# Three short products ahead of six chunks, and activations without a shifted low part, in a hybrid decoder layer

## The chip, the cores and the metric

The kernel runs on one core of one Trainium2 chip. The metric is the device time of one execution in microseconds. Three runs of the kernel before gave a median of 1507.69 us (1507.61 to 1507.84).

## What is computed

One decoder layer on 256 positions of width 2048, in float32: a norm, one wide input projection, two branches, a merge, an output projection, and a gated MLP, with a final norm.

```python
h = rms_norm(x, ln1)
qkv_a, beta_a, decay_a, z_a, qkv_b, gate_a, gate_b = split_columns(h @ w_in)
y_a = gated_deltanet(qkv_a, beta_a, decay_a, z_a, ...) @ w_branch_a      # 8 heads of 128, chunks of 64
q_b, k_b, v_b = jnp.split(qkv_b, 3, axis=-1)                             # 8 heads of 128, partial rotary
y_b = moba_attention(q_b, k_b, v_b) @ w_branch_b                         # causal over the one block of 256
merged = sigmoid(gate_a) * y_a + sigmoid(gate_b) * y_b
x = x + merged @ w_out
h = rms_norm(x, ln2)
u = causal_dwconv(h @ w_up, ffn_conv, ffn_conv_bias)                     # 2 x 5632 columns
u_gate, u_val = jnp.split(u, 2, axis=-1)
x = x + (silu(u_gate) * u_val) @ w_down
return rms_norm(x, final_norm)
```

## The kernel before

Activations lie transposed: features on the 128 partitions, the 256 positions along the free dimension, so that a 2048-wide activation is 16 tiles (k = 0 to 15) of 128 x 256. All large products are made from split numbers: a value is kept as a high part of the reduced float32 type and a low part that holds the rest. For each k three products are added up: high weights by high activation, high weights by low activation, low weights by high activation (the loop in `block`, L188 to L193; L110 is the instruction).

Weights come by one DMA queue (SyncE) in pieces of 1 MB into four raw buffers (`wraw`). ScalarE casts them to the high part (`wh`, L120), VectorE subtracts to get the low part (`wl`, L117), in two pieces of 1024 columns each. There are two buffers of each part. A *block* is 128 output columns: 16 k, 48 products of 256 columns. A *chunk* is two blocks (j = 0 and 1) into one PSUM tile, 96 products. The stages that are made of chunks are, in the order of time: the input projections of the delta rule (`ps_gdn`, `ps_z`), of the attention (`ps_moba`), the gates (`ps_gate`, 16 chunks), the two branch projections (`ps_br`, 16 chunks of half the length, as k runs to 7 alone), the output projection (`ps_wo`, 8 chunks), and the up-projection (`ps_up`, 44 chunks). The values of the attention (`ps_v`) and the down-projection (`pd`) have the activations as weights and stream 512 columns of the matrix.

While the chunks of the first stages run, small products of the delta rule and of the attention are put between them: `main_mm` counts the cost of the large products, and each time it comes to 1700 (`EVERY`) it lets each background item go one step on (`tick`). The place of these steps in TensorE's order depends on that count alone, not on time. In gate chunk 2 the last item ends; from there to the end TensorE runs the stages one after the other, with the two sums of squares of the second norm (`R2`, L98) between the output projection and the second chunk of the up-projection.

Where things lie is set by hand. `Parts` (L152 to L171) holds an activation as one row of elements: for each group of 8 k the high and low parts alternate, 256 elements each, and 64 elements are left over at the end of a group. `at(k, a)` gives the place of part `a` of tile `k`; the low part (a = 1) of the last k of a group (7 and 15) is moved on by `TURN` = 40 elements. `load_w` cuts the weights out of a buffer of 2048 + 64 elements from an offset `at`: 24 for most stages, and what `PLACE` says for two of them (8 for `ps_v`, 16 for `ps_wo`). The addresses of the built program, in bytes: the weights of the chunks start 32 past a multiple of 64, those of the output projection at a multiple of 64. The activations `hc`, `yca`, `ycb` and `h2` start 32 past a multiple of 64 too, the merged activations `mc` at a multiple of 64.

Of the kernel before, what the change touches and what calls it, by code (L numbers as in the profile page):

```python
# [11 lines left out]
F32 = mybir.dt.float32  # L12
# [7 lines left out]
P = 128  # L20
T = 256
D = 2048
KD = D // P
# [3 lines left out]
NF = DFF // P  # L27
EPS = 1e-6
EVERY = 1700
PLACE = {"v": 8, "wo": 16}  # L30
TURN = 40
GROUP = 8
ATT_SCALE = 128 ** -0.5
CONST_FIELDS = [
# [48 lines left out]
def layer_kernel(ctx: ExitStack, tc: tile.TileContext, xT, pos, cst, csel, ceye, vec, convw, ffw, bdv,  # L83
                 w_gdn, w_bd, w_moba, w_mv, w_gate, w_ba, w_bb, w_o, w_up, w_dn, fnorm, out):
    nc = tc.nc
    pe, act, dve, pool, sp = nc.tensor, nc.scalar, nc.vector, nc.gpsimd, nc.sync
# [5 lines left out]
    def r3(t, b):  # L92
        return t.rearrange("p (a b) -> p a b", b=b)
# [25 lines left out]
    def split(hi, lo, src):  # L119
        act.copy(hi, src)  # L120
        return low(hi, lo, src)
# [6 lines left out]
    def fetch(src, n=2048):  # L128
        raw = wpool.tile([P, 2048], F32, name="wraw", tag="wraw", bufs=4)
        sp.dma_start(raw[:, :n], src)  # L130
        return raw

    def load_w(src, n=2048, into=None, piece=1024, raw=None, at=0):
        raw = raw or fetch(src, n)
        wh, wl = into or [wpool.tile([P, 2048 + 64], F32R, name=t, tag=t)[:, at:at + 2048] for t in ("wh", "wl")]
        for o in range(0, n, piece):
            lows.append(split(wh[:, o:o + piece], wl[:, o:o + piece], raw[:, o:o + piece]))
        return wh[:, :n], wl[:, :n]
# [13 lines left out]
    class Parts:  # L152
# [6 lines left out]
        def at(self, k, a):  # L159
            return k // GROUP * self.size + (2 * (k % GROUP) + a) * T + TURN * (a and k % GROUP == GROUP - 1)  # L160

# [20 lines left out]
    def mmt(name):  # L182
        return pst[0].tile([P, 2, T], F32, name=name, tag="mm")

    def sdt(name):
        return pst[1].tile([P, 512], F32, name=name, tag="sd")

    def block(ps, j, w, x, kt, k0=0, k1=None):  # L188
        wh, wl = (r3(t, P) for t in w)
        for k in range(k0, k1 or kt):  # L190
            for w_, a in ((wh, 0), (wh, 1), (wl, 0)):
                main_mm(ps[:, j], w_[:, k, :], x.one(k, a), j == k == a == 0 and w_ is wh,
                        k == kt - 1 and w_ is wl)  # L193

    def chunk(blocks, x, kt, name, raws=(None, None), piece=1024, steps=((0, 0, None), (1, 0, None))):
        ps = mmt("ps_" + name)
        ws = {}
        for j, k0, k1 in steps:
            if j not in ws:
                ws[j] = load_w(blocks[j], kt * P, raw=raws[j], piece=piece, at=PLACE.get(name, 24))  # L200
            block(ps, j, ws[j], x, kt, k0, k1)
        return ps

    def join(dst, ps, r):
        with tc.high_priority():
            dve.tensor_tensor(dst, ps, r, op=ALU.mult)  # L206

    def scaled(xv, lnv, k, x):
        for j in range(xv.shape[1]):
            act.activation(x.one(k + j, 0), xv[:, j, :], AF.Identity, scale=lnv[:, k + j:k + j + 1])  # L210
            dve.scalar_tensor_tensor(x.one(k + j, 1), xv[:, j, :], lnv[:, k + j:k + j + 1],
                                     x.one(k + j, 0).bitcast(F32), op0=ALU.mult, op1=ALU.subtract)
# [9 lines left out]
    def both(r):  # L222
        return r[:, None, :].to_broadcast([P, 2, T])
# [3 lines left out]
    hc = Parts(hp, KD, "hc", tag="hc")  # L227
# [31 lines left out]
    raws = [fetch(w) for w in (w_gdn[2], w_gdn[3])]  # L259
# [18 lines left out]
    sp.dma_start(eye, ceye)  # L278

    ps_k0 = chunk([w_gdn[2], w_gdn[3]], hc, KD, "gdn", raws)  # L280


# [18 lines left out]
    R1b = both(R1)  # L301
# [21 lines left out]
    m = m_st.enter_context(tc.tile_pool(name="m", bufs=2, reuse_waits="tile"))  # L323
# [275 lines left out]
    def pair(w, i):  # L599
        return [w[2 * i], w[2 * i + 1]]  # L600

    for gr in range(4):
        h0 = 2 * gr
        kq = g.tile([P, 2, 2, T], F32, name="kq", bufs=1)
        v = g.tile([P, 2, T], F32, name="v", bufs=1)
        for a, t in enumerate((kq[:, 1], kq[:, 0], v)):
            if gr == 0 and a < 2:
                ps = (ps_q0, ps_k0)[a]
            else:
                ps = chunk(pair(w_gdn, 4 * gr + a), hc, KD, "gdn")  # L610
            conv4(t, ps, 8 * a + h0)
            if gr == 0 and a == 1:
                bg.append(decay())
        yv = ya[:, h0:h0 + 2, :]
        join(yv, chunk(pair(w_gdn, 4 * gr + 3), hc, KD, "z"), R1b)
        act.activation(yv, yv, AF.Silu)
        while gr == 0 and bg:
            tick()
        bg.append(gdn(h0, kq, v))
        if gr == 3:  # L620
            bg.append(rotary())
            sp.dma_start(ffv, ffw)
# [46 lines left out]
    for gr in range(4):  # L669
        h0 = 2 * gr  # L670
        qk = []
        for a in range(2):
            ps = chunk(pair(w_moba, 2 * gr + a), hc, KD, "moba")
# [3 lines left out]
        if gr % 2 == 0:  # L677
            ps = [mmt("ps_v").rearrange("p a b -> p (a b)") for _ in range(2)]
            for q_ in range(4):
                wh, wl = (r3(t, 512) for t in load_w(w_mv[2 * gr + q_], at=PLACE["v"]))  # L680
                for i in range(2):
# [9 lines left out]
        v = v4[:, :, (gr % 2) * T:(gr % 2 + 1) * T]  # L691
# [8 lines left out]

    gts = gp.tile([P, 16, 2, T], F32, name="gts")
    for c in range(16):
        join(gts[:, c], chunk(pair(w_gate, c), hc, KD, "gate"), R1b)
        act.activation(gts[:, c], gts[:, c], AF.Sigmoid)
    while bg:
        tick()
# [10 lines left out]

    m_st = ExitStack()
    m = m_st.enter_context(tc.tile_pool(name="mp", bufs=1, reuse_waits="tile"))
    mc = Parts(m, KD, "mc")  # L720
    for c in range(8):
        bts = [yp.tile([P, 2, T], F32, name="bt", bufs=3) for _ in range(2)]
        join(bts[0], chunk(pair(w_ba, c), yc[0], H, "br"), gts[:, c])
        ps = chunk(pair(w_bb, c), yc[1], H, "br")
# [18 lines left out]
    h2 = Parts(hp, KD, "h2", tag="hc")  # L743
    for c in range(8):
        steps = ((0, 0, KD - 2), (1, 0, 8), (0, KD - 2, KD), (1, 8, KD))
        ps = chunk(pair(w_o, c), mc, KD, "wo", **({} if c else dict(piece=512, steps=steps)))
        if c % 2 == 0:
            s = slice(2 * c, 2 * c + 4)
            sp.dma_start(x1[:, s, :], xT[:, s, :])
        xc = x1[:, 2 * c:2 * c + 2, :]  # L750
        dve.tensor_tensor(xc, xc, ps, op=ALU.add)
        scaled(xc, ln2v, 2 * c, h2)
        if c == 0:
            act.activation(sqa, xc, AF.Square)
        else:
            sq = b.tile([P, 2, T], F32, name="sq2")
            act.activation(sq, xc, AF.Square)
            if c < 7:
                pool.tensor_tensor(sqa, sqa, sq, op=ALU.add)
# [6 lines left out]
    ak = bk.enter_context(tc.tile_pool(name="ak", bufs=1, side="right", reuse_waits="tile"))  # L766
    acts = ak.tile([P, NF, T], F32, name="acts")
    for c in range(NF):
        ps = chunk([w_up[c], w_up[NF + c]], h2, KD, "up")
        un = b.tile([P, 2, T], F32, name="unf")  # L770
        join(un, ps, R2b)
        t = b.tile([P, 2, T], F32, name="cvf")
        for j in range(2):
            w = ffv[:, j * NF + c, :]
            act.activation(t[:, j, :], un[:, j, :], AF.Identity, scale=w[:, 2:3], bias=w[:, 3:4])
            for d in (1, 2):
                dve.scalar_tensor_tensor(t[:, j, d:], un[:, j, :T - d], w[:, 2 - d:3 - d], t[:, j, d:],
                                         op0=ALU.mult, op1=ALU.add)
        sg = b.tile([P, T], F32, name="sg")
        act.activation(sg, t[:, 0, :], AF.Silu)  # L780
        pool.tensor_tensor(acts[:, c, :], sg, t[:, 1, :], op=ALU.mult)
# [128 lines left out]
```

## Time and profile before

| | |
|---|---|
| runs, median (range) | 1507.69 us (1507.61 to 1507.84) |
| profiled execution, its own time | 1512.56 us |
| its span, first to last instruction | 1510.8 us |
| TensorE products (PE), busy | 1494.0 us, 99% |
| VectorE / ScalarE / GpSimd busy | 968.2 / 721.1 / 121.1 us |
| moved by DMA | 277.23 MB, mean 184 GB/s |
| granted TensorE clock | 0.995 |

PE is the product on TensorE, PEld the load of its weights. Matmuls are pipelined, so the duration of a product (some 280 ns) is longer than the step from one start to the next; steps are read from the start times. In the timeline, products of the same form that follow each other stand in one row with their number (x2). In the chain of waits a piece is a stretch of one engine's work with nothing waited for between, with its start, its length and its number of instructions. "wh", "wl" are the high and low weights, "hc", "h", "mc", "yca", "ycb" the activations.

### The profile page before, as it was taken

What the parts mean: (1) busy time and instruction counts of PE and PEld (TensorE: products, weight loads), DVE (VectorE), ACT (ScalarE), POOL (GpSimd) and SP (SyncE); (2) the same over time, 40 slices, a digit from 0 to 9 for tenths busy, and PEclk for the clock granted to TensorE, in tenths of its full rate; (3) what the DMA queues carried; (4) which work ended last, traced back from release to release, by engine and by line L of the source; (5) the groups of instructions that cost most, each with busy time, mean ns of one, the idle gap of its engine ahead of it and who ended that gap; (6) DMA issues with size and microseconds to landing.
All of it is one profiled execution on the core that took longest, in us unless ns stands there. A gap on an engine that the chain in (4) does not pass through costs nothing.

```text
span 1510.8 us, 26931 instructions
## 1 busy us (share of the span) xinstructions
PE 1494.0 (99%) x11471; PEld 1434.1 (95%) x11471; DVE 968.2 (64%) x1373; ACT 721.1 (48%) x948; POOL 121.1 (8%) x133
## 2 busy tenths in 40 slices
PE   9999999999999999999999999999999999999998
PEld 8999999998999999999999999999999998888886
DVE  7988695886665445666666666666666665555554
ACT  5655363434474433445455444454444554444444
POOL 0001011042120000110100000000000000000000
PEclk9999999999999999999999999999999999999999
DMA  9445444444336553568555555555555554555552
GB/s 341 171 148 184 171 153 162 152 158 144 136 126 209 195 182 125 183 215 303 195 171 195 193 195 187 183 189 196 195 184 184 192 195 167 195 196 195 195 195 84
DMA packets 45657, 277.23 MB, mean 184 GB/s; under 512 B 5504, under 2 KB 6992, under 8 KB 15456
## 3 DMA queue, kind: packets, MB, share of 16 engines
q1 hardware_dynamic: 43712, 270.98, 52.0%
q0 software_dynamic: 960, 2.36, 0.5%
q10 hardware_dynamic: 864, 2.16, 0.4%
q8 instruction: 90, 1.47, 0.4%
q14 instruction: 31, 0.25, 0.0%
HBM read 271.68 MB, written 3.80 MB: 182 GB/s over the span
## 4 chain that ended last, share of the span: by engine, by line
PE 90%; DVE 5%; ACT 2%; DMA 1%; issue 1%; SPq 0%; DVEq 0%; POOLq 0%; ACTq 0%
PE ps_up L110 32%; PE pd L98 16%; PE ps_gate L110 11%; PE ps_gdn L110 8%; PE ps_wo L110 6%; PE ps_br L110 5%; PE ps_moba L110 3%; PE ps_z L110 3%; PE ps_v L110 2%; DVE wl L117 2%; ACT wh L120 1%; DMA wraw<-in_w_gdn 1%; PE g L98 1%; PE py L552 0%; PE pu L558 0%
## 5 line engine op out<-in xcount | busy, mean ns | idle before, releaser
L117 DVE TENSOR_TENSOR wl<-wraw,wh 128x1024 fp32r<-128x1024 f32 (+1 forms) x500 | 607.1, 1248 | 221.6 <-ACT wh L120 221.0
L120 ACT CAST wh<-wraw 128x1024 fp32r<-128x1024 f32 (+1 forms) x500 | 497.5, 1040 | 481.2 <-PE ps_up L110 171.8
L110 PE MATMUL ps_up<-h,wh 128*128 128x256 f32 x2816 | 489.7, 279 | 0.0
L110 PEld LDWEIGHTS ps_up<-h,wh 128*128 128x128 f32 x2816 | 429.4, 189 | 0.1
L110 PE MATMUL ps_up<-h,wl 128*128 128x256 f32 x1408 | 392.4, 279 | 0.0
L110 PEld LDWEIGHTS ps_up<-h,wl 128*128 128x128 f32 x1408 | 264.3, 188 | 0.0
L110 PE MATMUL ps_gate<-hc,wh 128*128 128x256 f32 x1024 | 181.2, 281 | 0.0
L110 PEld LDWEIGHTS ps_gate<-hc,wh 128*128 128x128 f32 x1024 | 157.5, 190 | 0.0
L110 PE MATMUL ps_gate<-hc,wl 128*128 128x256 f32 x512 | 143.5, 281 | 0.2 <-DVE wl L117 0.2
L98 PE MATMUL pd<-wl,ah 128*128 128x512 f32 x336 | 130.8, 389 | 0.0
L98 PE MATMUL pd<-wh,al 128*128 128x512 f32 x336 | 130.8, 389 | 0.0
L110 PE MATMUL ps_gdn<-hc,wh 128*128 128x256 f32 x704 | 126.7, 283 | 0.0
L110 PEld LDWEIGHTS ps_gdn<-hc,wh 128*128 128x128 f32 x704 | 108.9, 191 | 0.9 <-ACT wh L120 0.4
L110 PE MATMUL ps_gdn<-hc,wl 128*128 128x256 f32 x352 | 99.8, 284 | 0.8 <-DVE wl L117 0.8
L110 PEld LDWEIGHTS ps_gate<-hc,wl 128*128 128x128 f32 x512 | 96.8, 189 | 0.4 <-DVE wl L117 0.4
L98 PE MATMUL pd<-wh,ah 128*128 128x512 f32 x336 | 92.8, 391 | 0.0
L110 PE MATMUL ps_moba<-hc,wh 128*128 128x256 f32 x512 | 92.8, 282 | 0.0
L206 DVE TENSOR_TENSOR unf<-ps_up,R 128x512 f32<-128x512 f32 x44 | 30.4, 691 | 95.7 <-PE ps_up L110 95.7
L110 PE MATMUL ps_wo<-mc,wh 128*128 128x256 f32 x512 | 89.2, 279 | 0.0
L110 PEld LDWEIGHTS ps_moba<-hc,wh 128*128 128x128 f32 x512 | 78.5, 189 | 0.2
L110 PEld LDWEIGHTS ps_wo<-mc,wh 128*128 128x128 f32 x512 | 78.1, 189 | 0.0
L98 PEld LDWEIGHTS pd<-wh,al 128*128 128x128 f32 x336 | 63.1, 188 | 13.2
(420 smaller groups left out, 1963.5 us busy)
## 6 DMA issues: line engine op xcount, KB each, us to landing
wraw<-in_w_up SPq DMA_DIRECT2D x88, 1024.0 KB, 4.9
wraw<-in_w_dn SPq DMA_DIRECT2D x44, 1024.0 KB, 4.9
wraw<-in_w_gate SPq DMA_DIRECT2D x32, 1024.0 KB, 4.9
wraw<-in_w_gdn SPq DMA_DIRECT2D x30, 1024.0 KB, 5.0
wraw<-in_w_moba SPq DMA_DIRECT2D x16, 1024.0 KB, 4.9
wraw<-in_w_o SPq DMA_DIRECT2D x16, 1024.0 KB, 5.3
wraw<-in_w_mv SPq DMA_DIRECT2D x8, 1024.0 KB, 5.0
wraw<-in_w_ba SPq DMA_DIRECT2D x16, 512.0 KB, 3.5
```

The source lines that it names most:

```text
L98: pe.matmul(ps, a, b, start=(start and i == 0), stop=(stop and i == n - 1), **kw)
L110: pe.matmul(ps, a, b, start=start, stop=stop, skip_group_check=True)
L117: return (eng or dve).tensor_tensor(lo, src, hi.bitcast(F32), op=ALU.subtract)
L120: act.copy(hi, src)
L206: dve.tensor_tensor(dst, ps, r, op=ALU.mult)
```

## The change

Three things are changed.

`TURN` becomes 0: the low part of the tiles 7 and 15 lies where the others do, right behind its high part. The 64 spare elements stay.

A tile of 8 elements is allotted ahead of the merged activations, so that `mc` starts 32 bytes later, and the output projection loses its entry in `PLACE`, so that its weights start at element 24 in place of 16, also 32 bytes later.

`chunk` gets the chunk's number. For the chunks that `KICKS` names (gate 7, output projection 1, up-projection 1, 12, 23 and 34) it loads the first block's weights as usual and then issues three products of 128 columns ahead of the block's own: the first 128 columns of the high weights by the first 128 columns of the high activation, each with start and stop set, into a PSUM tile of the small pool that nothing reads.

```diff
-PLACE = {"v": 8, "wo": 16}
-TURN = 40
+PLACE = {"v": 8}
+TURN = 0
+KICKS = {"gate": (7,), "wo": (1,), "up": (1, 12, 23, 34)}
...
-    def chunk(blocks, x, kt, name, raws=(None, None), piece=1024, steps=((0, 0, None), (1, 0, None))):
+    def chunk(blocks, x, kt, name, raws=(None, None), piece=1024, steps=((0, 0, None), (1, 0, None)), c=None):
         ps = mmt("ps_" + name)
         ws = {}
+        if c in KICKS.get(name, ()):
+            ws[0] = load_w(blocks[0], kt * P, raw=raws[0], piece=piece, at=PLACE.get(name, 24))
+            idle = sdt("kick")
+            for _ in range(3):
+                pe.matmul(idle[:, :P], ws[0][0][:, :P], x.one(0, 0)[:, :P], start=True, stop=True)
         for j, k0, k1 in steps:
...
-        join(gts[:, c], chunk(pair(w_gate, c), hc, KD, "gate"), R1b)
+        join(gts[:, c], chunk(pair(w_gate, c), hc, KD, "gate", c=c), R1b)
...
+    m.tile([P, 8], F32, name="before_mc")
     mc = Parts(m, KD, "mc")
...
-        ps = chunk(pair(w_o, c), mc, KD, "wo", **({} if c else dict(piece=512, steps=steps)))
+        ps = chunk(pair(w_o, c), mc, KD, "wo", c=c, **({} if c else dict(piece=512, steps=steps)))
...
-        ps = chunk([w_up[c], w_up[NF + c]], h2, KD, "up")
+        ps = chunk([w_up[c], w_up[NF + c]], h2, KD, "up", c=c)
```

TensorE's order at the head of up-projection chunk 1, with the numbers of the buffers, before:

```order
L110 MATMUL ps_up_8394<-h2_7399,wh_8453 128x256 x2
L110 MATMUL ps_up_8394<-h2_7399,wl_8454 128x256
L110 MATMUL ps_up_8519<-h2_7399,wh_8522 128x256 x2
L110 MATMUL ps_up_8519<-h2_7399,wl_8523 128x256
L110 MATMUL ps_up_8519<-h2_7399,wh_8522 128x256 x2
```

and with the change:

```order
L111 MATMUL ps_up_8403<-h2_7404,wh_8462 128x256 x2
L111 MATMUL ps_up_8403<-h2_7404,wl_8463 128x256
L203 MATMUL kick_8537<-h2_7404,wh_8531 128x128 x3
L111 MATMUL ps_up_8528<-h2_7404,wh_8531 128x256 x2
L111 MATMUL ps_up_8528<-h2_7404,wl_8532 128x256
L111 MATMUL ps_up_8528<-h2_7404,wh_8531 128x256 x2
```

The last two rows of chunk 0 are followed by the three added products and then by chunk 1 as it was. The other five places read the same way with their own names. On VectorE, ScalarE, GpSimd and SyncE every row stands where it stood, and so does every other row of TensorE.

## The prediction

> **What bounds the kernel now.** I read the page first, then the chain of waits, then the timeline of TensorE alone.
>
> ```profile
> span 1510.8 us, 26931 instructions
> PE 1494.0 (99%) x11471; PEld 1434.1 (95%) x11471; DVE 968.2 (64%) x1373; ACT 721.1 (48%) x948; POOL 121.1 (8%) x133
> PE 90%; DVE 5%; ACT 2%; DMA 1%; issue 1%; SPq 0%; DVEq 0%; POOLq 0%; ACTq 0%
> 448.24 139.15 PE ps_gate L110 x1198
> 679.93 89.14 PE ps_wo L110 x768
> 775.66 484.43 PE ps_up L110 x4182
> 1268.46 235.03 PE pd L98 x1035
> ```
>
> The first three lines say that TensorE sets the time; the last four are the longest pieces of the chain of waits, in which products follow each other with no wait. One product of 256 columns takes 484.43 / 4182 = 0.1158 us in the up-projection, 0.1161 in the gates and in the output projection. A 512-column product of the last stage takes 0.2271, or 2 x 0.1135. So the 256-column stages run about 2% above the pace of the last stage, and no wait is named for it. The starts of one up-projection block (48 products, three per k) show where the 2% is:
>
> ```profile
> 904.09 0.40 PE L110 MATMUL ps_up<-h,wh 128*128 128x256 f32 x2
> 904.44 0.40 PE L110 MATMUL ps_up<-h,wh 128*128 128x256 f32 x2
> ...
> 906.56 0.40 PE L110 MATMUL ps_up<-h,wh 128*128 128x256 f32 x2
> ...
> 906.92 0.39 PE L110 MATMUL ps_up<-h,wh 128*128 128x256 f32 x2
> 907.26 0.39 PE L110 MATMUL ps_up<-h,wh 128*128 128x256 f32 x2
> ...
> 909.30 0.39 PE L110 MATMUL ps_up<-h,wh 128*128 128x256 f32 x2
> ...
> 909.65 0.40 PE L110 MATMUL ps_up<-h,wh 128*128 128x256 f32 x2
> ```
>
> The first column is the start; a row stands for the two wh products of one k, the wl product lies between. From k = 0 to k = 7 the seven steps from 904.09 to 906.56 take 2.47 us, 0.353 per k: call it the **slow pace**, 0.1176 per product. From k = 8 to k = 15 the seven steps from 906.92 to 909.30 take 2.38 us, 0.340 per k: the **fast pace**, 0.1133. At 909.65 the next block starts slow again. The pace turns at k = 7 and at k = 15, the two places at which the low part of the activation lies 40 elements further on, and nowhere between. A pace, once there, stays until such a shifted product or an interruption. The present kernel so spends half its products in each pace: a block takes 2.83 + 2.73 = 5.56 us.
>
> **The change part by part.**
>
> *No low part lies further on.* No product is added or removed, and addresses cost nothing by themselves; what goes is the turn at k = 7 and 15. A stretch then keeps the pace with which it began. An all-fast chunk of 32 k takes 32 x 0.340 = 10.88 us against 11.12 now, 0.24 less; an all-slow one 32 x 0.353 = 11.30, about 0.17 more. All hangs on which pace each stretch gets.
>
> *Merged activations and their weights.* Both move by 32 bytes together (the merged tensor by 8 elements, its weights from place 16 to 24), so their offset to each other is as before. The output projection's 0.1161 per product at the old place and the up-projection's 0.1158 at the new one are one pace mix, so I take nothing. The cover is this agreement alone: if the new place were bad, the most it can cost is the slow pace throughout, 8 chunks x 0.17 = 1.4 us.
>
> *The three products ahead of six chunks.* 18 products of 128 columns, into a bank that nobody reads. Each waits for the first half of its high weights, as the chunk's first product does; behind it on TensorE stands the whole chunk, and the join on VectorE waits for that. The wait should be empty, since ScalarE waits for TensorE there and not the other way round:
>
> ```profile
> ACT wh L120 <- PE ps_up L110: 168.4, 84, 3.6
> 800.00:900.00 100.00, 100.00 (x866) 100.00 (x865) 63.17 (x83) 48.93 (x65) 6.64 (x9) 1.00 0.55 190
> ```
>
> No product of this form and type is in the trace. The nearest for its duration are the 64-column groups of the delta rule, where loading weights and not streaming sets the step: eight of them from 141.23 to 142.04 in the rows below, 0.81 / 8 = 0.10 each. The bounds are 0.06 (half a 256-column product, if only streaming counted) and 0.118 (a slow one). I take 0.11, near the upper end, since the group shows that half the columns don't halve the step: 18 x 0.11 = 2.0 us (1.1 to 2.1), all on the path.
>
> What pace do they leave behind? That is the disputed cost, and there are two kinds of near rows. Behind a stall of TensorE (first and last line here: the wait that ends it, and the second of its seven cases shown, then the last):
>
> ```profile
> PE ps_br L110 <- DVE wl L117: 1.7, 7, 0.3
> 636.64 0.38 PE L110 MATMUL ps_br<-yca,wl 128*128 128x256 f32 x1 [0.24 <-DVE wl L117]
> ...
> 637.22 0.39 PE L110 MATMUL ps_br<-yca,wh 128*128 128x256 f32 x2
> ...
> 638.24 0.39 PE L110 MATMUL ps_br<-yca,wh 128*128 128x256 f32 x2
> 671.59 0.39 PE L110 MATMUL ps_br<-yca,wl 128*128 128x256 f32 x1 [0.24 <-DVE wl L117]
> ...
> 672.16 0.39 PE L110 MATMUL ps_br<-yca,wh 128*128 128x256 f32 x2
> 672.50 0.39 PE L110 MATMUL ps_br<-yca,wh 128*128 128x256 f32 x2
> 672.84 0.39 PE L110 MATMUL ps_br<-yca,wh 128*128 128x256 f32 x2
> ```
>
> From 637.22 to 638.24 three k take 1.02, from 672.16 to 672.84 two take 0.68: fast, whatever the pace was before; all seven stalls of the branches end so (one longer stall in the first stage ended slow). Behind a group of short products in plain fp32, and behind the four fp32 products of the norm:
>
> ```profile
> 141.23 1.00 PE L552 MATMUL py<-Tm,aq 128*128 128x64 f32 x8
> 142.04 0.36 PE L110 MATMUL ps_gdn<-hc,wl 128*128 128x256 f32 x1
> 142.24 0.40 PE L110 MATMUL ps_gdn<-hc,wh 128*128 128x256 f32 x2
> 142.59 0.40 PE L110 MATMUL ps_gdn<-hc,wh 128*128 128x256 f32 x2
> 142.94 0.40 PE L110 MATMUL ps_gdn<-hc,wh 128*128 128x256 f32 x2
> ...
> 774.64 1.02 PE L98 MATMUL R<-sq,ones 128*128 128x256 f32 x4
> ...
> 775.85 0.40 PE L110 MATMUL ps_up<-h,wh 128*128 128x256 f32 x2
> 776.21 0.40 PE L110 MATMUL ps_up<-h,wh 128*128 128x256 f32 x2
> ```
>
> 0.35 per k: slow. Of 21 such groups of 64 columns 14 end slow; the first is shown, the last starts at 380.27. The added products share with the stall that they are of the reduced type and that the array stands partly idle while the next weights come in (0.057 of streaming in a step of 0.11); they share with the short groups only the step. I take the stall as the nearer row: the pace behind them is fast. Both ends stay for the range.
>
> **The sum, all stretches fast from their kick on:**
> - Up-projection, chunks 1 to 43: 43 x 0.24 = 10.3 off. Chunk 0 runs slow behind the norm's products at 774.64 until the first kick: 0.15 on.
> - Output projection, 8 chunks x 0.24 = 1.9 off; it inherits the fast pace from the last stall, so its own kick changes nothing there.
> - Gates, from the stall ahead of 448.24 to 587.39: 139.15 / 11.12 = 12.5 chunks x 0.24 = 3.0 off.
> - Branches, 16 half chunks x 0.12 = 1.9 off, less what the seven stalls take back. They end when VectorE is done, so a block ahead of a stall that is 0.11 shorter only waits 0.11 longer: 7 x 0.11 = 0.8. Net 1.1 off.
> - Ahead of the gates some 2500 products stand between interruptions and keep whatever pace each leaves. Their mix is about half now. I take 0; the bounds are 2500 x 0.0022 = 5.5 either way.
> - Kicks: 2.0 on.
>
> 10.3 - 0.15 + 1.9 + 3.0 + 1.1 - 2.0 = 14.1 us off. The profiled execution took 1512.56 us, its span 1510.8 plus 1.8 around it, and lies 4.9 above the median of the runs. The difference carries over: 1507.69 - 14.1 = **1493.6 us**. What is late next: nothing soon. At 10.88 us per chunk VectorE goes from 63% to 65% busy and the DMA engines from 0.55 to 0.56.
>
> **A rule that speaks against it.** The slow pace shows in the starts from 904.09 to 906.56. The Trainium skill, "TensorE: Matmul & The Clock Gate", part 2, step 1, says that TensorE reads its weights and its moving operand through two independent ports, so that loading the next weights takes nothing from the running product. By it no offset between the two could matter, and the change would be worth its 18 products alone, 1509.7 us. The turn at exactly the two shifted places speaks against the rule here.
>
> **The rivals.**
> 1. *The kicks leave the slow pace.* Place: from gate chunk 7 on. For it: the rows behind 141.23. Against: the seven stalls. Gates 9 x 0.17 - 3.5 x 0.24 = 0.7 on, output projection 7 x 0.17 - 0.24 = 1.0 on, up 43 x 0.17 + 0.15 = 7.5 on, branches 1.1 off (their stalls still make them fast), kicks 2.0 on: +10.1, so **1517.8, slower**. It turns the sign once more than about 18 of the 43 up chunks are slow too: 43 x 0.24 = 10.3 less the other 2.8, by 0.41 each.
> 2. *The kicks toggle the pace.* For it: a shifted product does just that, in both directions. The four in the up-projection then give 11 fast, 11 slow, 11 fast and 10 slow chunks: -5.3 + 3.6 + 0.15 = -1.6; gates 0.7, output 1.0, branches -1.1, kicks 2.0: +1.0, **1508.7, the same**.
> 3. *The fast pace doesn't hold for ten chunks.* In the present kernel no 256-column stretch is longer than 24 products without a turn, so nothing here shows that it holds for 1056. For holding: 1035 products of the last stage at 2 x 0.1135. Half of each up stretch lost: 21 x 0.41 = 8.6 less, **1502**.
> 4. *The interruptions ahead of the gates leave the slow pace in nearly all.* +5 there, with mixed kicks around 1511.
> 5. *The pace has nothing to do with the place* and turns every eight k by itself. Against it: the interruptions change it. +2.0: **1509.7**.
>
> **How the numbers follow.** The forecast 0.56, rival 1 0.18, 2 0.08, 3 0.10, 4 0.04, 5 0.04. A difference of 0.2%, 3.0 us, is about what runs of this kernel can tell from no change. Faster by more: 0.56 + 0.10 = 0.66; the same: 0.08 + 0.04 = 0.12; slower: 0.18 + 0.04 = 0.22. The forecast's own range is 1488 to 1499 (the 5.5 of the early stages on the low side, half of it on the high side, and the price of the kicks). The range that holds the time 8 times in 10 is 1488.5 to 1514: it takes in rivals 2 to 5 and leaves out most of rival 1.
>
> **What would show it.** The starts of TensorE in the up-projection: 0.340 per k from the first kick to the last chunk, and its 4182-product piece down from 484.4 to about 474; behind each kick the first few k tell whether the pace is 0.340 or 0.353. The output projection's 768 products down from 89.1 to 87.2. The kicks' own steps of 0.11, with no wait ahead. In the branches, seven stalls a little longer than 0.24. The forecast is wrong if any up stretch reads 0.353 per k, or if the pace changes inside a stretch with nothing ahead of it.

## The result, and the profile after

The changed kernel took 1497.8 us in the median of four runs (1495.58 to 1501.34), the kernel before 1507.76 (1507.61 to 1510.16): a ratio of 0.9932, interval 0.991 to 0.9955. So it is faster by 10.0 us (7 to 14), or 0.7%. The forecast was 1493.6, with 1488 to 1499 as its own range and 1488.5 to 1514 as the one that holds the time 8 times in 10; the measured time lies in both. The profiled execution took 1498.51 us, 14.05 less than that of before. Its page has these three lines for those shown of before:

```profile
span 1496.7 us, 26967 instructions
PE 1478.6 (99%) x11489; PEld 1418.4 (95%) x11489; DVE 967.8 (65%) x1373; ACT 720.9 (48%) x948; POOL 121.2 (8%) x133
PE 91%; DVE 4%; DMA 2%; ACT 1%; issue 1%; SPq 0%; DVEq 0%; ACTq 0%
```

TensorE still sets the time, with 18 products more and 15.4 us less of work. The chain of waits (start, length, number of instructions) shows at which stages:

```profile
486.14 97.99 PE ps_gate L111 x864
...
777.06 119.75 PE ps_up L111 x1056
...
1254.38 235.03 PE pd L99 x1035
```

The pieces of the up-projection end at the triples now. 119.75 / 1056 = 0.1134 us per product, against 0.1158 before; the gates behind their triple have 97.99 / 864 = 0.1134, against 0.1161. The last stage is as it was, 235.03. The fast pace holds through. The timeline of TensorE, in the same chunk in which the prediction showed the turn at k = 7:

```profile
903.79 0.39 PE L111 MATMUL ps_up<-h,wh 128*128 128x256 f32 x2
...
905.49 0.39 PE L111 MATMUL ps_up<-h,wh 128*128 128x256 f32 x2
```

From 903.79 to 905.49 five k (4 to 9 of the chunk's second block) take 1.70, or 0.340 each. Around the triple ahead of gate chunk 7 the same view reads:

```profile
485.36 0.39 PE L111 MATMUL ps_gate<-hc,wh 128*128 128x256 f32 x2
...
485.70 0.44 PE L203 MATMUL kick<-hc,wh 128*128 128x128 f32 x3
485.98 0.45 PE L111 MATMUL ps_gate<-hc,wh 128*128 128x256 f32 x2
...
486.39 0.39 PE L111 MATMUL ps_gate<-hc,wh 128*128 128x256 f32 x2
...
486.73 0.39 PE L111 MATMUL ps_gate<-hc,wh 128*128 128x256 f32 x2
```

From 485.70 to 486.39, the triple and one k, are 0.69 us, 0.35 more than a k alone: the triple's own 0.28, and 0.07 by which the first product behind it steps later. The pace was fast ahead of the triple (0.34 from 485.36 to 485.70), and is 0.34 per k again behind it (from 486.39 to 486.73). That holds for all six triples of this profile: each was entered fast and left fast. So this profile shows what a triple costs, 6 x 0.35 = 2.1 us, and nothing that one is good for. With that the experiments begin.

### The profile page after: what moved, and what is told of

It is laid out like the page before. It is cut to its first block, busy times and chain, and to the rows that moved or that the text cites. A ratio compares the mean times of both kernels' runs of the same rounds, so it can differ in the third digit from the quotient of the medians.

```text
span 1496.7 us, 26967 instructions
## 1 busy us (share of the span) xinstructions
PE 1478.6 (99%) x11489; PEld 1418.4 (95%) x11489; DVE 967.8 (65%) x1373; ACT 720.9 (48%) x948; POOL 121.2 (8%) x133
## 4 chain that ended last, share of the span: by engine, by line
PE 91%; DVE 4%; DMA 2%; ACT 1%; issue 1%; SPq 0%; DVEq 0%; ACTq 0%
PE ps_up L111 32%; PE pd L99 16%; PE ps_gate L111 11%; PE ps_gdn L111 8%; PE ps_wo L111 5%; PE ps_br L111 5%; PE ps_moba L111 4%; PE ps_v L111 3%; PE ps_z L111 3%; DVE wl L118 2%; DMA wraw<-in_w_gdn 1%; ACT wh L121 1%; DMA x<-in_xT 1%; PE g L99 1%; PE py L558 1%
## 5 line engine op out<-in xcount | busy, mean ns | idle before, releaser
L111 PE MATMUL ps_up<-h,wh 128*128 128x256 f32 x2816 | 479.7, 276 | 0.0
L111 PEld LDWEIGHTS ps_up<-h,wh 128*128 128x128 f32 x2816 | 424.2, 188 | 0.1
L111 PE MATMUL ps_gate<-hc,wh 128*128 128x256 f32 x1024 | 176.8, 278 | 0.0
```

The lines of the kernel that those rows point to most:

```text
L111: pe.matmul(ps, a, b, start=start, stop=stop, skip_group_check=True)
```

## The experiments

The stages in us, from the profiled execution of each kernel: each from the start of its first product to that of the next stage's first, the last one to the start of its last product; "early" is all from TensorE's first product to the gates. The first two rows are the kernels already shown. The runs of the others stood beside runs of the kernel before on the same chip, which had medians of 1508.11 (the next four rows), 1510.39 (the four behind them) and 1507.38 (a single run, the last two rows).

| | early | gates | branches | output | up | last | its own time |
|---|---|---|---|---|---|---|---|
| before | 393.1 | 193.1 | 92.5 | 89.8 | 490.3 | 243.2 | 1512.56 |
| changed kernel | 394.0 | 189.0 | 92.0 | 88.7 | 481.2 | 243.2 | 1498.51 |
| again | 390.4 | 190.6 | 91.6 | 88.5 | 481.2 | 243.2 | 1495.90 |
| no triples | 391.1 | 190.2 | 91.3 | 89.0 | 479.8 | 243.2 | 1495.14 |
| triples alone | 390.3 | 191.9 | 92.5 | 90.2 | 491.8 | 243.2 | 1510.28 |
| a shifted product in four chunks | 391.1 | 190.5 | 91.7 | 88.1 | 498.4 | 243.1 | 1513.34 |
| a shifted product ahead of the up-projection | 394.2 | 190.3 | 91.7 | 88.0 | 479.8 | 243.2 | 1497.58 |
| the same with one triple | 391.3 | 190.2 | 91.7 | 89.5 | 480.1 | 243.2 | 1496.34 |
| one, two, four products | 390.7 | 195.6 | 91.8 | 89.2 | 498.5 | 243.2 | 1519.36 |
| old place, no triples | 393.1 | 188.7 | 91.7 | 91.1 | 498.6 | 243.2 | 1516.80 |
| old place, with triples | 391.5 | 190.6 | 91.4 | 88.5 | 481.2 | 243.2 | 1496.79 |
| weights apart | 394.3 | 188.7 | 91.7 | 91.6 | 479.8 | 243.2 | 1499.69 |

An up-projection all in the fast pace, without triples, is 479.8; all in the slow pace, 498.5. That span of 18.7 us is what the experiments play with.

**The changed kernel again.** No edit.

> The changed kernel once more, unaltered. Theory (a stretch keeps the pace that its last interruption left; the late stages are all fast, and the runs differ by the pace that the interruptions of the first stages happen to leave): 1495 to 1502 us, and in its profile the late stages as before: up-projection 481.2 us, output projection 88 to 89, gates about 189, with the differences to the other profile ahead of the gates. Rival (the runs differ because the fast pace breaks somewhere in the late stages): a stretch of 0.353 us per k in the up-projection or the output projection.

Median 1495.94 (1495.48 to 1498.09), ratio 0.9915 (0.9898 to 0.9932). Every stretch from gate chunk 3 on, but for parts of the branches, is fast as in the first profile, and all triples were again entered fast. The profile differs from the first ahead of the gates (390.4 for 394.0), as the theory had it, and in the gates (190.6 for 189.0), which it had at about 189. The granted clock differs in both places, as is shown further down.

**Without the triples.**

```diff
-KICKS = {"gate": (7,), "wo": (1,), "up": (1, 12, 23, 34)}
+KICKS = {}
```

> The changed kernel without any of the 18 added products. Theory A (the added products make a slow stretch fast, and are needed where an interruption leaves the slow pace): if the norm's fp32 products leave the fast pace as in the profile of the changed kernel, 6 x 0.35 = 2.1 us less than it; if they leave the slow pace as in the profile before, the 43 up chunks are slow and it is 43 x 0.41 - 2.1 = 15.5 us more. Theory B (the added products do nothing; without a shifted part every stretch is fast by itself): 2.1 us less in every run, some 1495.5.

Median 1495.45 (1495.14 to 1495.76), ratio 0.9909 (0.9893 to 0.9925): the gain stands without one triple. The chain of waits of this kernel:

```profile
446.42 136.06 PE ps_gate L111 x1198
...
768.59 473.98 PE ps_up L111 x4182
```

473.98 / 4182 = 0.1133. This is the 474 that the prediction had named, and it comes without triples: 4182 products keep the pace that they were entered with. The stage is 1.4 us shorter than with its four triples, 4 x 0.35. So in the profiles of the changed kernel the gain is that of the unshifted low parts (with the new place, as will be seen), and the triples cost their 2.1 us. Over the whole kernel the two intervals don't tell the medians of 1495.45 and 1495.94 apart.

**The triples alone.** The old shift, the old place, and the triples:

```diff
-PLACE = {"v": 8}
-TURN = 0
+PLACE = {"v": 8, "wo": 16}
+TURN = 40
...
-    m.tile([P, 8], F32, name="before_mc")
```

> The kernel before with the 18 added products as its only change (shift of 40 elements, places and the merged tensor as before). Theory A and B alike (the shift turns the pace every eight k, so no chunk can stay fast): 2.1 us more than before, 1509.8. Rival (the gain comes from the added products themselves): about 10 us less than before.

Median 1510.71 (1509.41 to 1517.2), ratio 1.002 (1.0007 to 1.0033): about 2.6 us slower than the kernel before, near the price of six triples. The up-projection keeps its mixed pace; its first piece in the chain of waits is

```profile
778.50 122.40 PE ps_up L111 x1056
```

or 0.1159 per product. The rival falls with that: triples alone gain nothing. With the shift in, nothing that a triple leaves behind lasts longer than to the next k = 7. But there is a trace of what it leaves: in the kernel before, the blocks of the up-projection begin slow and turn fast at k = 7; here, behind the triple at 778.05, they begin fast (0.34 per k from 779.09 to 780.79) and turn slow at k = 7, and so it goes on.

**A shifted product behind each stretch.** To learn what a triple does to a slow stretch, one has to make a slow stretch. The changed kernel, and ahead of up-projection chunks 2, 13, 24 and 35 one product of 256 columns into a tile that nobody reads, whose activation begins 40 elements further on:

```diff
+FLIPS = {"up": (2, 13, 24, 35)}
...
+        if c in FLIPS.get(name, ()):
+            ws[0] = load_w(blocks[0], kt * P, raw=raws[0], piece=piece, at=PLACE.get(name, 24))
+            o = x.at(0, 0) + 40
+            pe.matmul(sdt("flip")[:, :T], ws[0][0][:, :P], x.flat[:, o:o + T], start=True, stop=True)
```

> The changed kernel with one more product of 256 columns, at an activation 40 elements further on and into an unused bank, ahead of up chunks 2, 13, 24 and 35, each one chunk behind an added triple. Theory A (one shifted product turns the pace, the turned pace lasts until the next triple, and the triple makes it fast again): chunks 2 to 11, 13 to 22, 24 to 33 and 35 to 43 slow, 11.30 us each, chunks 12, 23, 34 fast, 39 x 0.41 + 4 x 0.12 = 16.5 us more than the changed kernel. Theory B (the triples do nothing): the shifted products alone turn the pace: chunks 2 to 12 slow, 13 to 23 fast, 24 to 34 slow, 35 to 43 fast, 22 x 0.41 + 0.5 = 9.5 us more. Rival (a pace does not last for ten chunks): slow stretches that end with nothing ahead of them.

Median 1514.28 (1512.66 to 1517.97), ratio 1.004 (1.0029 to 1.0052). The pieces of the up-projection in its chain of waits alternate:

```profile
774.76 10.95 PE ps_up L112 x96
...
785.82 113.07 PE ps_up L112 x960
898.89 0.28 PE kick L204 x3
899.17 10.96 PE ps_up L112 x96
910.14 0.12 PE flip L208
910.25 113.07 PE ps_up L112 x960
```

A chunk right behind a triple takes 10.95 or 10.96 (fast, 10.88, and the 0.07 of its first product), the ten behind a shifted product take 113.07, or 0.1178 per product: slow. Four added products, 4 x 0.12 us of work in all, cost the stage 17.2 us (481.2 to 498.4); theory A had 16.5. This shows three things at once. A single shifted product makes a fast stretch slow, four times of four. The slow pace holds for 960 products. And the triples at 898.89, 1023.32 and 1147.76 were entered slow and left fast, three of three. They can turn the pace, only not where it is fast already.

**A slow start of the up-projection.** The prediction had chunk 0 slow behind the products of the norm. In the changed kernel it isn't, so a shifted product ahead of chunk 0 (and no triples) was to make it so:

```diff
-KICKS = {"gate": (7,), "wo": (1,), "up": (1, 12, 23, 34)}
+KICKS = {}
+FLIPS = {"up": (0,)}
```

> No added triples, and one shifted 256-column product into an unused bank ahead of up chunk 0, so that the norm's second group of fp32 products, ten k later, is entered slow. Theory A1 (that group keeps the pace with which it is entered: slow in the kernel before, fast in the changed one): all 44 up chunks slow at 11.31, up-projection about 479.8 + 44 x 0.43 = 498.7 us, 1514.4 in all. Theory A2 (such a group leaves the fast pace unless chance has it otherwise): a third of chunk 0 slow alone, 1495.8.

Median 1497.08 (1493.71 to 1500.43), ratio 0.9907 (0.9883 to 0.9931), the up-projection at 479.8. The timeline of TensorE shows the last slow k of its first stretch (0.35 from 769.05 to 769.40), the second group of norm products, and what stands behind it:

```profile
769.05 0.40 PE L112 MATMUL ps_up<-h,wh 128*128 128x256 f32 x2
...
769.40 0.40 PE L112 MATMUL ps_up<-h,wh 128*128 128x256 f32 x2
...
769.99 1.03 PE L100 MATMUL R<-sq,ones 128*128 128x256 f32 x4
...
771.32 0.39 PE L112 MATMUL ps_up<-h,wh 128*128 128x256 f32 x2
...
771.66 0.39 PE L112 MATMUL ps_up<-h,wh 128*128 128x256 f32 x2
```

The four fp32 products were entered slow and left fast, 0.34 per k. So A1, that the group keeps the pace with which it is entered, falls. In the kernel before, the same group was entered slow and left slow. So such a group may turn the pace or not, and what it does isn't fixed by its form. One difference stays open: here it stands ahead of a wl product, in the middle of a k, and in the kernel before ahead of a wh pair.

**The same with one triple**, ahead of up-projection chunk 1:

```diff
-KICKS = {}
+KICKS = {"up": (1,)}
```

> The same with one added triple, ahead of up chunk 1. Theory A (a triple makes a slow stretch fast): at most chunk 0 slow, 0.12 + 0.43 + 0.35 = 0.9 us more than without both, 1496.4. Theory B (triples do nothing): as the kernel without the triple, 0.35 more.

Median 1495.27 (1492.38 to 1498.86), ratio 0.9894 (0.9866 to 0.9922), the up-projection at 480.1, 0.35 more than without. The norm had made it fast before the triple came. The run says nothing more on what a triple does.

**One, two and four products.** Is it the number? The shifted product ahead of chunks 2, 13 and 24, and a kick of one product ahead of chunk 12, of two ahead of 23, of four ahead of 34; no other kicks:

```diff
-KICKS = {"gate": (7,), "wo": (1,), "up": (1, 12, 23, 34)}
+KICKS = {"up": (12, 23, 34)}
+FLIPS = {"up": (2, 13, 24)}
...
-            for _ in range(3):
+            for _ in range({12: 1, 23: 2, 34: 4}[c]):
```

> Shifted products ahead of up chunks 2, 13 and 24, and ahead of chunks 12, 23 and 34 one, two and four of the 128-column products in place of three. If it is the short products' step that restores the pace, two and four do it (chunks 12 and 34 to 43 at 10.9) and one may; if the number three matters (the phase that it adds up to), some of chunks 12, 23 and 34 stay at 11.31. A start that stays slow at 12 is turned fast by the shifted product at 13.

One execution, 1519.36. The chain of waits:

```profile
446.08 141.37 PE ps_gate L112 x1198
...
904.55 11.36 PE ps_up L112 x96
916.02 113.06 PE ps_up L112 x960
1029.26 10.94 PE ps_up L112 x96
1040.32 113.07 PE ps_up L112 x960
1153.79 113.12 PE ps_up L112 x960
```

Behind one product the chunk takes 11.36, slow; behind two, 10.94, fast; behind four, 113.12 for 960 products, slow to the end of the stage. With the triples of the run with a shifted product in four chunks: two and three turned a slow stretch fast, one and four did not. Each of one, two and four stands on one case. Of the two readings on record the first, by which two and four both do it, falls with the four; the number matters. The shifted products ahead of chunks 2 and 24 turned a fast stretch slow, as the four before had done. The one ahead of chunk 13 came into a slow stretch and did not turn it. In the kernel before, the shifted low part at k = 7 turns slow to fast in nearly every block of the up-projection, and the one at k = 15 in most blocks of the gates; those at 453.46 and 682.36 do not. What such a product does to a slow stretch isn't fixed by its form.

The first line was not looked for. All 1198 gate products are at 0.1180, slow, where the same piece without triples in the other run was 136.06. Both pieces begin at the same stall of TensorE in gate chunk 3. The starts behind it, in this kernel,

```profile
446.08 0.39 PE L112 MATMUL ps_gate<-hc,wl 128*128 128x256 f32 x1 [0.37 <-DVE wl L119]
446.30 0.40 PE L112 MATMUL ps_gate<-hc,wh 128*128 128x256 f32 x2
...
446.65 0.40 PE L112 MATMUL ps_gate<-hc,wh 128*128 128x256 f32 x2
```

are 0.35 apart, and in the kernel without triples, behind a stall of the same 0.37 at the same product, 0.34. So a stall may leave either pace, and here it cost 141.37 - 136.06 = 5.3 us. This kernel had no triple ahead of gate chunk 7. Of the ten profiles here without the shift it is the only one in which this stall left the slow pace.

**The old place of the merged activations, without triples.** Of the change only the unshifted low parts are left:

```diff
-PLACE = {"v": 8}
+PLACE = {"v": 8, "wo": 16}
-KICKS = {"gate": (7,), "wo": (1,), "up": (1, 12, 23, 34)}
+KICKS = {}
...
-    m.tile([P, 8], F32, name="before_mc")
```

> No shift and no triples, with the merged activations and the output projection's weights both at their old place (each 32 bytes earlier). Theory (only their offset to each other and to the rest of the stream counts, and it is the same): output projection 88 to 89 us, 10.88 per chunk as in the kernel without triples. Rival (the old place is worse): chunks of 11.1 to 11.3, 1.8 to 3.4 us more.

One execution, 1516.80, 21 us above the kernel without triples, from which it differs only by the place. The theory on record falls; its rival had the pace of the output projection, but not that it lasts. The chain of waits has the two pieces

```profile
674.68 90.45 PE ps_wo L111 x768
771.81 492.55 PE ps_up L111 x4182
```

90.45 / 768 = 0.1178 and 492.55 / 4182 = 0.1178: slow from the first product of the output projection to the last of the up-projection, through both norm groups. The timeline shows where it began:

```profile
673.83 0.39 PE L111 MATMUL ps_br<-ycb,wh 128*128 128x256 f32 x2
...
674.17 0.39 PE L111 MATMUL ps_br<-ycb,wh 128*128 128x256 f32 x2
...
674.52 0.40 PE L111 MATMUL ps_wo<-mc,wh 128*128 128x256 f32 x2
...
674.87 0.40 PE L111 MATMUL ps_wo<-mc,wh 128*128 128x256 f32 x2
```

0.34 per k in the branches, 0.35 from the first product of `mc` on. Nothing lies between but the step of 32 bytes (modulo 64) in where activation and weights begin; in the activation a low part moved by 40 elements (160 bytes) makes the same step. With everything at the new place, the pace did not turn at this border in any of the seven profiles; here and in the next run it did. It is no property of the old place: in the kernel before, half of nearly every output chunk was fast there, and in the next run most of it is.

**The old place with the triples.**

```diff
-KICKS = {}
+KICKS = {"gate": (7,), "wo": (1,), "up": (1, 12, 23, 34)}
```

> The changed kernel, but with the merged activations and the output projection's weights left at their old place, as in the run without triples that was slow from the output projection to the end of the up-projection. The triples are all there: ahead of gate chunk 7, output chunk 1, up chunks 1, 12, 23 and 34. Theory K (a triple makes a slow stretch fast, whatever the place): output chunk 0 at 11.31, chunks 1 to 7 at 10.9; the norm's products and up chunk 0 at 11.3 if the change of place behind the norm turns the pace once more, 10.9 if not; from up chunk 1 on fast; up-projection 480 to 482 us, time 1494 to 1501 us. Theory P (at the old place the output projection is slow whatever a triple does; those of the up-projection still work): output chunks 1 to 7 at 11.3, stage at 91 us, up-projection 481 to 482, time 1496 to 1503. Theory R (behind the old place neither kind of triple works): output 91, up 498 to 500, time 1515 to 1520.

One execution, 1496.79. The chain of waits:

```profile
674.64 11.31 PE ps_wo L111 x96
686.23 76.24 PE ps_wo L111 x672
775.38 119.75 PE ps_up L111 x1056
```

Output chunk 0 is slow again, 11.31, turned by the step of 32 bytes. The triple ahead of chunk 1 makes the rest fast, 76.24 / 672 = 0.1135, and the up-projection inherits it: the step back to the usual place, which stands behind a norm group, turned nothing. The first of the three readings on record holds. The place and the triple ahead of output chunk 1 each prevent the same slow stretch, worth 20 us between these two runs; either alone is enough.

**The weights 32 bytes apart from the activation.** The new place for `mc`, the old one for the output projection's weights, no triples:

```diff
-PLACE = {"v": 8}
+PLACE = {"v": 8, "wo": 16}
-KICKS = {"gate": (7,), "wo": (1,), "up": (1, 12, 23, 34)}
+KICKS = {}
```

> No triples; the merged activations at the new place, and the output projection's weights alone 32 bytes back at their old place, so that the two lie 32 bytes further apart than in any other run. Theory M (only the place of the streamed activations counts, and a change of it between two stages turns the pace): the place stays the branches', so the output projection stays fast, chunks at 10.9, stage at 88 to 89 us; up-projection 479.8; time 1494 to 1500. Theory O (the place of the weights against the activations counts): the offset changes at the first output product, so the pace turns there: output chunks at 11.3, stage at 91 us, and the offset changes back at the up-projection: fast again at 480, or slow at 498; time 1497 to 1503, or 1515 to 1520.

One execution, 1499.69. The chain of waits:

```profile
675.88 90.88 PE ps_wo L111 x768
773.25 473.98 PE ps_up L111 x4182
```

The output projection is slow, 90.88 / 768 = 0.1183, from its first product on, and the up-projection is fast, which is theory O in the first of its two forms. So the place of the weights counts as well as that of the activations. This pace is a third one: single steps in it run from 115 to 123 ns, while those of the slow pace lie between 117 and 119 for the most part, and the chunk takes 11.36 in place of 11.31. Whether it could turn to fast within the stage wasn't tried.

## Why the prediction was right, and where it was not

The sum and what the profiles show, by stage, in us. The triples' price is put to the stage in which they stand; "measured" is the changed kernel less the kernel before, for the gates from its second profile, for the reason that follows:

| stage | predicted | measured |
|---|---|---|
| up-projection | -10.3 + 0.15 + 1.3 = -8.8 | -9.1 |
| output projection | -1.9 + 0.3 = -1.6 | -1.1 |
| gates | -3.0 + 0.3 = -2.7 | -2.6 |
| branches | -1.1 | -0.6 |
| ahead of the gates | 0 | +0.9 |
| sum | -14.1 | -12.5 |

**"The difference carries over."** The two profiled executions differ by 14.05, which looks like the sum on the point, and the medians by 10.0 in the first comparison and 12.2 in the second. The profiles agree with the sum partly by luck. At two places, near 80 us and in gate chunk 0, products run at a lower granted clock in some executions and not in others. The windows in the profile of before, and then the second place in that of the changed kernel (columns: window and its length, busy time and number on PE, PEld, DVE, ACT, POOL, granted clock, DMA share, GB/s):

```profile
76.00:84.00 8.00, 8.00 (x44) 6.58 (x44) 4.78 (x17) 2.76 (x4) 1.04 (x1) 0.77 0.40 131
84.00:90.00 6.00, 6.00 (x41) 6.00 (x41) 5.86 (x17) 3.57 (x4) 0.00 (x0) 0.74 0.34 97
400.00:404.00 4.00, 2.12 (x19) 1.94 (x19) 4.00 (x4) 2.58 (x3) 3.52 (x3) 1.00 0.38 111
404.00:410.00 6.00, 6.00 (x38) 5.91 (x38) 3.44 (x6) 1.97 (x3) 0.00 (x0) 0.72 0.63 221
```

```profile
400.00:404.00 4.00, 2.80 (x25) 2.59 (x23) 4.00 (x4) 1.82 (x3) 3.89 (x3) 1.00 0.14 29
404.00:410.00 6.00, 5.22 (x42) 5.14 (x43) 4.39 (x7) 2.73 (x4) 0.55 (x1) 1.00 0.61 212
```

In gate chunk 0, behind a wait of 1.9 us (2.0 in the changed kernel), the kernel before had a clock of 0.72 and the changed one 1.00. The products that ran low stepped by 213 to 214 ns in place of 113. The second profile of the changed kernel has the low clock there too (0.72), and its gates are 1.6 us longer: 190.6 in place of 189.0. From like to like the gates gained 2.6 and not 4.1, and the pair 12.5 and not 14.0. Near 80 us both first profiles ran low, with 0.75 from 84 to 90 in the changed kernel, and its second one at 1.00. In the 19 runs of the kernel before that stood beside the first experiments the time goes with the mean clock: eleven at 0.999 have a mean of 1508.0, two at 0.995, the clock of the profiled one, 1511.8 and 1512.3. The prediction had noticed the 4.9 us between profile and median and passed over them. The windows of before explain them: the clock that lacks there, 0.23 x 8 + 0.26 x 6 + 0.28 x 6, is an estimated 5.1 us. The Trainium skill, "TensorE: Matmul & The Clock Gate", part 1, describes half the clock after an idle window of about 3.4 us whose phase doesn't follow the kernel. The rows agree in the half (213 ns for 113) and in that it is low in one execution and full in the next at the same place; they differ in what stands ahead of it: a wait of 1.9 us in gate chunk 0, and near 80 us no wait at all, as TensorE is busy for all of the 8 us from 76 to 84. What spreads the changed kernel's own runs (1495.58 and 1501.34 at one clock of 0.998) no profile shows.

**The mechanism: right.** The slow pace ends with the shift, and 43 chunks of 10.88 are what the up-projection shows. The fast pace holds for the whole stage (rival 3 falls: 4182 products at 0.1133 without a triple).

**"Chunk 0 runs slow behind the norm's products": wrong.** Both norm groups left the pace fast in the changed kernel, in its second profile and without triples. The group at 774.64 was entered slow (0.35 from 773.93 to 774.28), which the prediction did not look at; every norm group there that was entered fast left fast, where it can be seen. Entered slow, it left slow in the kernel before, with the triples alone and at the old place without triples, and fast in the two runs with a slow start. The worth was small, 0.15 + 0.24 = 0.4 us.

**"The pace behind them is fast": right for three products, and for a reason that the prediction had no row for.** The changed kernel itself couldn't show it. Three triples entered slow and left fast in the run with a shifted product in four chunks, and one at the old place; all those entered fast left fast. Rivals 1 and 2 fall with that. But the argument, by the nearest row, does not carry: the stall that it took as nearest leaves either pace (gate chunk 3, and two of the seven branch stalls below), and a kick of one or of four products left the slow pace standing. That three is a number that works is luck, as far as the prediction's argument goes. Their price came out as said, 2.1 for 2.0, though not in equal steps of 0.11: the three step by 58, 112 and 114 ns, and the first product behind them by 60 more than its usual 113.

**"Its own kick changes nothing there" and the output projection's price.** The kick changed nothing, as said. But the step has a second half that the prediction didn't see: "merged activations ... so I take nothing", with 1.4 us at the most. At the old place, without the shift and without triples, 21 us are lost, since the turn at the first product of `mc` lasts through the output projection and the whole up-projection. The bound was taken for one stage; the pace doesn't end with a stage. That "addresses cost nothing by themselves" holds only while they keep their place modulo 64, as the run with the weights apart shows again (0.1183). With the triple ahead of output chunk 1 the new place is worth the 0.4 us by which chunk 0 was slow at the old one, near the nothing that was taken; without the triples it is worth 21.

**The output projection's gain: 0.5 short.** Output chunk 1 has a wait that before had not:

```profile
DVE x L758 <- DMA x<-in_xT: 3.9, 1, 3.9
```

```profile
693.35 0.38 PE L111 MATMUL ps_wo<-mc,wl 128*128 128x256 f32 x1 [0.38 <-DVE wl L118]
```

VectorE waits 3.9 us for the residual's transfer, which it joins to chunk 0 (before it was 1.2); behind that in its order stands the subtraction that makes the next low weights, and TensorE waits for those. Chunk 1 takes 11.61 in place of 10.88 and its 0.35 for the triple: 0.4 us. "What is late next: nothing soon" missed this. TensorE's wait there differs from one execution to the next: 0.38 here, 0.12 in the second profile, 1.00 in the kernel without triples.

**The branches: half of the gain.** Seven stalls cost 2.1 us where they had cost 1.7; 0.8 more was reckoned with. What lacks is the pace: the pieces between the stalls, from the chain of waits,

```profile
598.24 8.41 PE ps_br L111 x69
609.99 8.13 PE ps_br L111 x69
621.51 8.41 PE ps_br L111 x69
```

take 8.41 behind the first and third stall, slow, and 8.13 where the stall left the pace fast. "All seven stalls end so" was true of one profile.

**Ahead of the gates** 0.9 us were lost between the two first profiles, both with the low clock near 80 us, where 0 had been taken, within the 5.5 that were given. With the full clock there the second profile took 390.4 and the triples alone, whose early stages are those of the kernel before, 390.3: nothing lost. Of the products of the attention's projections some 70% stepped slow, against some 58% before, of the delta rule's 71% against 62% (61% in the second profile). Rival 4 has little for it: neither its "nearly all" nor its 5. **Rival 5** falls by the runs with the shifted product and at the old place: a product 40 elements further on, or a step of 32 bytes, turns the pace, and without either it lasts for 4182 products.

**"A rule that speaks against it."** By what the prediction drew from the two independent ports of the Trainium skill ("TensorE: Matmul & The Clock Gate", part 2, step 1), the time would have been 1509.7. The measured pace goes against that twice more: one product with its activation 40 elements further on made the next 960 products take 0.1178 in place of 0.1133, and 32 bytes in the weights alone 0.1183. Whether it is the ports that hold the pace no run shows.

## What to carry to other kernels

Where products of one form run at two paces, read the starts one by one and look for the product at which the pace turns; four per cent on each product may be inherited from one odd address hundreds of products earlier. Keep the place of activations and weights, modulo 64 bytes, the same across stage borders (steps of 32 and 160 bytes are all that was tried here), and price a turn by all that follows until the next interruption, not by its own stage. Products that are put in against a slow stretch can only be judged on a slow stretch: make one on purpose, and vary their number.

## What was not expected of the hardware

The pace of 256-column products of reduced float32 has a memory. A stretch takes 0.1133 or 0.1178 us per product and keeps either for 960 products and more. A single product whose activation lay 32 bytes off (modulo 64) turned fast to slow between plain products six times of six, four in one run and two in another. Three short products turned slow to fast four times of four, and two in the one case tried; one product or four did not, one case each. What in the chip holds the pace, and why a stall of the same length at the same place ends now fast and now slow, stays open.
